# Latent attention: value products on half columns in fp32, with the sums of probabilities on GpSimd

## The chip, the cores and the metric

The program runs on one core of one Trainium2 chip. The metric is the device time of one execution in microseconds, as the median of several executions of the same kernel. TensorE (PE) does the matrix products, VectorE (DVE) and ScalarE (ACT) the elementwise work, GpSimd (POOL) a little of it; SyncE (SP) issues most transfers.

## The reference, cut to what matters

A trunk of two layers over 1024 positions of width 1024. The first layer mixes tokens by multi-head latent attention (12 heads, keys of 64+32, values of 64), the second by a sliding window; both have four cross-attention heads beside them, an output projection and a squared-ReLU MLP. The change lies in the causal attention of the first layer:

```
sc = einsum('bqhd,bkhd->bhqk', q_blk, k) * scale
sc = where(k_idx <= t_idx, sc, NEG)
p  = softmax(sc, axis=-1)
o  = einsum('bhqk,bkhd->bqhd', p, v)
```

The softmax is computed as exp(scores minus the row's maximum), a product with the values, and a division by the sum of the exponentials. All of it has the accuracy of fp32.

## The kernel before

**Tiles.** Scores are computed transposed: a block is 128 keys (on partitions) by up to 512 queries. Group G=0 holds queries 0 to 511, G=1 queries 512 to 1023, so a head has 4 blocks (k=0 to 3) of group 0 and 8 (k=0 to 7) of group 1. A block on the diagonal (k >= 4G) has only the columns from (k-4G)*128 on, so widths are 512, 384, 256 and 128. Step n of the main loop is one block of one head (`seq`, 12 steps a head); the list `blocks` gives the order, `blocks_end` that of the last head.

**A step.** `scores` makes three products into one PSUM bank `pss` (high and low parts of q and k, in the fp32r format), adds the mask on DVE where the block is on the diagonal, and takes the exponential on ACT into `p`. The row's maximum comes in as a 97th row of q, which `row_max` (PE product `psx`, minimum of the negated scores on DVE) and `max_row` (a transpose, a split, two small DMAs) prepare for a later head; the table `WHEN` says at which steps. `head_tiles` loads and splits q and k of the head after next.

**Values.** `values` is called for the block three steps back and, for its second part, five steps back (`LV`, `LB`). Blocks of group 1, and (0, 3) of the first eleven heads, are used whole (`whole`): one fp32 product of `vf` (64 columns of values and 64 of ones) with `p`, so that the lower half of the bank `pso` holds the output and the upper half the sums of probabilities. The other blocks of group 0 are split into `ph` (ACT) and `pl` (DVE) and take three fp32r products with `vh` and `vl`. `v_tiles` and `v_full` make these value tiles for each head.

**After a group.** ACT copies 65 rows of `pso` into `on`; DMAs take the output back into `qn` and the row of sums into `den`. For groups of heads (0 to 5, 6 to 9, 10) `rc_split` takes reciprocals of `den`, writes them to DRAM and reads them back spread over 64 partitions (`rb`, two buffers), in the queue of POOL for the first two groups; `rc_mul` multiplies one output tile in each odd step. The last head is divided straight from PSUM by `last_o`, its group 1 at once, its group 0 in the output projection (`wo_phase`).

**Order.** Each engine works through one queue, in an order fixed when the program is built: a planner takes the instructions by their place in the program and puts each where its inputs and a free buffer are to be had. `tc.issue_after(x)` ties what is issued inside it behind instruction x in the queue of x's engine. A wait at the head of a queue holds up all that stands behind it.

Of the kernel before, what the change touches and what calls it, by code (L numbers as in the profile page):

```python
# [9 lines left out]
F32 = mybir.dt.float32  # L10
# [9 lines left out]
P = 128  # L20
# [35 lines left out]
def trunk(  # L56
# [943 lines left out]
    vbufs = []  # L1000
    for i in range(2):
        vb = (at.tile([P, 4, 128], F32R, name=f"vh{i}"), at.tile([P, 4, 64], F32R, name=f"vl{i}"))
        vbufs.append(vb)
    vfs = [at.tile([P, NT, 128], F32, name=f"vf{i}") for i in range(2)]
    for vf in vfs:
        nc.gpsimd.memset(vf[:, :, 64:128], 1.0)

    def v_tiles(h):

        vh, vl = vbufs[h % 2]  # L1010
        src = v[:, 0:4, h * 64 : (h + 1) * 64]
        if h < 2:
            nc.gpsimd.memset(f32(vh[:, :, 64:128]), 1.0)
        nc.scalar.activation(vh[:, :, 0:64], src, AF.Copy)
        nc.vector.tensor_tensor(vl, src, f32(vh[:, :, 0:64]), ALU.subtract)

    blocks = [(1, 0), (0, 0), (1, 4), (0, 1), (1, 5), (0, 2), (1, 6), (0, 3), (1, 7), (1, 1), (1, 2), (1, 3)]

    def whole(h, G, k):
        return G == 1 or (k == 3 and h < H - 1)  # L1020

    blocks_end = [(1, k) for k in (0, 4, 5, 6, 7, 1, 2, 3)] + [(0, k) for k in range(4)]

# [3 lines left out]
    probs, po_, masked = {}, {}, []  # L1027

    def width(G, k):
        return 512 - max(0, k - 4 * G) * P  # L1030

    def scores(h, G, k):

        qh, ql, kh, kl = bufs_[h % 3]
        c0 = 512 - width(G, k)
        ks = slice(k * P, (k + 1) * P)
        qs = slice(G * 512 + c0, G * 512 + 512)
        diag = k >= 4 * G
        ps = ps1(f"pss{h}_{G}_{k}")[:, c0:]

        def mm(o, a, b, **kw):
            return lambda: nc.tensor.matmul(o, a, b, skip_group_check=True, **kw)  # L1042

        mms = [mm(ps, kh[:, ks], qh[:, qs], start=True, stop=False)]
        mms.append(mm(ps, kh[:, ks], ql[:, qs], start=False, stop=False))
        mms.append(mm(ps, kl[:, ks], qh[:, qs], start=False, stop=True))

        def then():
            if diag:
                masked[0:1] = [nc.vector.tensor_tensor(ps[:, 0:P], ps[:, 0:P], dmaskT, ALU.add).ins]  # L1050
            p = at.tile([P, 512], F32, tag="p", bufs=5, name=f"p{h}_{G}_{k}")
            masked[1:] = [nc.scalar.activation(p[:, c0:], ps, AF.Exp, scale=SC).ins]  # L1052
            if whole(h, G, k):
                probs[(h, G, k)] = p
                return
            ph = at.tile([P, 512], F32R, tag="ph", bufs=3, name=f"ph{h}_{G}_{k}")
            pl = at.tile([P, 512], F32R, tag="pl", bufs=3, name=f"pl{h}_{G}_{k}")
            split(p[:, c0:], ph[:, c0:], pl[:, c0:])
            probs[(h, G, k)] = (ph, pl)

        return mms, then

    def values(h, G, k, late):

        vh, vl = vbufs[h % 2]
        c0 = 512 - width(G, k)
        order = [b[1] for b in blocks_of(h) if b[0] == G]
        first, last = k == order[0], k == order[-1]
        mms = []

        def mm(o, a, b, **kw):
            mms.append(lambda: nc.tensor.matmul(o, a, b, skip_group_check=True, **kw))  # L1072

        if first and not late:
            po_[(h, G)] = ps1(f"pso{h}_{G}")
        po = po_[(h, G)]
        if whole(h, G, k):
            if late:
                return [], lambda: None
            mm(po[:, c0:], vfs[h % 2][:, k, :], probs.pop((h, G, k))[:, c0:], start=first, stop=last)  # L1080
        elif late:
            mm(po[:, c0:], vh[:, k, :], probs.pop((h, G, k, "late"))[:, c0:], start=False, stop=last)
        else:
            ph, probs[(h, G, k, "late")] = probs.pop((h, G, k))
            mm(po[:, c0:], vh[:, k, :], ph[:, c0:], start=first, stop=False)
            mm(po[0:64, c0:], vl[:, k, :], ph[:, c0:], start=False, stop=False)
            last = False

        def then():
            if not last:  # L1090
                return
            r = slice((h % 2) * 64, (h % 2) * 64 + 64)
            if h == H - 1:
                if G:
                    last_o(G, at.tile([64, 512], F32, tag="on", bufs=2, name="rq1"))
                return
            on = at.tile([65, 512], F32, tag="on", bufs=2, name=f"on{h}_{G}")
            nc.scalar.activation(on, po[0:65], AF.Copy)
            nc.sync.dma_start(out=qn[h // 2][r, G * 512 : (G + 1) * 512], in_=on[0:64])
            c = [c for c in range(3) if h >= GRP[c]][-1]  # L1100
            d0 = (h - GRP[c]) * NT + 4 * G
            nc.sync.dma_start(out=den[c][d0 : d0 + 4, :], in_=on[64:65])

        return mms, then

    def last_o(G, tmp, js=range(4)):

        po = po_[(H - 1, G)]
        for j in js:
            c = slice(j * P, (j + 1) * P)  # L1110
            nc.vector.reciprocal(tmp[:, c], po[64:128, c])
            nc.vector.tensor_tensor(qn[5][64:128, G * 512 + j * P : G * 512 + (j + 1) * P], po[0:64, c], tmp[:, c], ALU.mult)
# [7 lines left out]
    def rc_pair(c, j, i):  # L1120

        rb = at.tile([P, 512], F32, tag="rb", bufs=2, name=f"rb{c}_{j}_{i}")
        for e in range(min(2, GRP[c + 1] - GRP[c] - 2 * j)):
            (nc.sync if c == 2 else nc.gpsimd).dma_start(out=rb[e * 64 : e * 64 + 64, :], in_=rc_d[c][2 * j + e, halves[i]].partition_broadcast(64))
        return rb

    def rc_split(c):
# [4 lines left out]
        (nc.sync if c == 2 else nc.gpsimd).dma_start(out=rc_d[c].rearrange("h (t p) -> (h t) p", p=P), in_=rc)  # L1132
# [33 lines left out]
    for n in range(len(seq) + LB):  # L1166
        ms, mv, then = [], [], []
        if n < len(seq):
            ms, then_s = scores(*seq[n])
        for lag, late in ((LB, True), (LV, False)):  # L1170
            if 0 <= n - lag < len(seq):
                a, b = values(*seq[n - lag], late)
                mv += a
                then.append(b)

        mix = []
        if ms and mv and P in [width(*seq[n - lag][1:]) for lag in (0, LV, LB)]:
            while ms and mv:
                mix += [ms.pop(0), mv.pop(0)]
        for f in mix + ms:  # L1180
            f()
        if n < len(seq):
            then_s()
# [1145 lines left out]
```

## Time and profile before

| | before |
|---|---|
| median of 3 runs | 2091.34 us (2090.69 to 2093.28) |
| profiled execution: span from first to last instruction | 2089.8 us |
| PE, weight loads, DVE, ACT, POOL busy, of the span | 99%, 81%, 71%, 53%, 7% |
| score products of the first layer, first to last start | 233.2 to 430.6 us |
| chain that ended last, by engine | PE 94%, DVE 3%, ACT 1%, DMA 1% |

The profile is one execution, and its times are from the span's start. The runs' times hold a little more than the span. Busy PE time is the union of overlapping records, since matrix products are pipelined. A record of the profile is one instruction; a line number is that of the kernel, and names such as `pso<-p,vf` give what is written and read.

### The profile page before, as it was taken

How to read it: one execution, taken by the hardware profiler on the slowest of the kernel's cores; microseconds unless marked ns; L12 is line 12 of the kernel's file. 1: busy time of each engine (PE TensorE's matmuls, PEld its weight loads, DVE VectorE, ACT ScalarE, POOL GpSimd, SP SyncE). 2: the span in 40 equal slices, each digit the busy share in tenths (PEclk: the TensorE clock that was granted, in tenths of full speed). 3: DMA queues.
4: the chain of work that ended last, by engine and by line, in shares of the span. 5: the costliest groups of instructions: out<-in, count | busy, mean ns of one | idle time of the engine just before them, and what ended most of it. 6: DMA issues, size and time to landing. Idle time of an engine off the chain costs nothing.

```text
span 2089.8 us, 28906 instructions
## 1 busy us (share of the span) xinstructions
PE 2072.6 (99%) x9744; PEld 1692.2 (81%) x9744; DVE 1475.7 (71%) x2978; ACT 1109.4 (53%) x2396; POOL 148.6 (7%) x265
## 2 busy tenths in 40 slices
PE   9999999999999999999999999999999999999998
PEld 6988777778888888888888888778888888888887
DVE  8766778775977777976558534666977776976565
ACT  7554466666745544444445435766755544444453
POOL 1001001000000000000001133420000000000000
PEclk9999999999999999999999999999999999999999
DMA  6302223342444546944433534542344446944332
GB/s 225 104 1 77 63 65 93 105 149 81 142 152 150 167 152 233 332 129 152 143 118 108 146 101 124 142 130 84 128 152 164 161 144 233 324 146 156 117 121 91
DMA packets 182228, 292.86 MB, mean 140 GB/s; under 512 B 17739, under 2 KB 72128, under 8 KB 182080
## 3 DMA queue, kind: packets, MB, share of 16 engines
q1 hardware_dynamic: 175584, 272.60, 41.5%
q0 software_dynamic: 5168, 15.80, 2.1%
q10 hardware_dynamic: 1328, 2.63, 0.4%
q8 instruction: 76, 1.25, 0.2%
q14 instruction: 72, 0.59, 0.1%
HBM read 187.60 MB, written 81.44 MB: 129 GB/s over the span
## 4 chain that ended last, share of the span: by engine, by line
PE 94%; DVE 3%; ACT 1%; DMA 1%; issue 1%; SPq 0%; POOL 0%; DVEq 0%; ACTq 0%
PE psy L1903 6%; PE psy L1901 6%; PE psy L1902 6%; PE psu L1565 5%; PE psu L1564 5%; PE psu L1563 5%; PE psz L1903 4%; PE psz L1902 4%; PE psz L1901 4%; PE psv L1565 4%; PE psv L1564 4%; PE psv L1563 4%; PE pso L1072 3%; PE pss L1042 3%; PE pswo L109 3%; PE pswo L111 3%
## 5 line engine op out<-in xcount | busy, mean ns | idle before, releaser
L99 ACT ACTIVATE g<-i 128x512 fp32r<-128x512 f32 x79 | 49.9, 631 | 104.6 <-PE psy L1902 51.8
L1901 PE MATMUL psy<-g 128*128 128x512 f32 x256 | 100.1, 391 | 0.0
L1902 PE MATMUL psy<-g 128*128 128x512 f32 x256 | 99.8, 390 | 0.0
L1903 PE MATMUL psy<-g 128*128 128x512 f32 x256 | 99.8, 390 | 0.0
L1052 ACT ACTIVATE p<-pss 128x512 f32<-128x512 f32 (+2 forms) x144 | 68.7, 486 | 58.5 <-DVE pss L1050 50.0
L100 DVE TENSOR_TENSOR g<-i,g 128x512 fp32r<-128x512 f32 x79 | 55.5, 702 | 51.0 <-ACT g L99 51.0
L1072 PE MATMUL pso<-p,vf 128*128 128x512 f32 (+3 forms) x214 | 87.8, 492 | 0.0
L99 ACT ACTIVATE i<-mr 128x512 fp32r<-128x512 f32 x78 | 47.8, 629 | 73.2 <-PE psy L1902 24.5
L99 ACT ACTIVATE uh<-i 128x512 fp32r<-128x512 f32 x66 | 41.6, 630 | 82.4 <-PE psz L1902 38.4
L100 DVE TENSOR_TENSOR uh<-i,uh 128x512 fp32r<-128x512 f32 x66 | 45.6, 691 | 47.3 <-ACT uh L99 47.2
L916 DVE CUSTOM_DVE_ANT_0 psx<-psx,wide 128x1024 f32<-128x1024 f32 (+6 forms) x88 | 66.7, 760 | 14.6 <-PE psx L909 14.4
L1903 PE MATMUL psz<-g 128*128 128x512 f32 x192 | 74.8, 389 | 0.0
L1901 PE MATMUL psz<-g 128*128 128x512 f32 x192 | 74.8, 389 | 0.0
L1902 PE MATMUL psz<-g 128*128 128x512 f32 x192 | 74.8, 389 | 0.0
L1462 ACT ACTIVATE mr<-mr,gcol 128x256 f32<-128x256 f32 (+1 forms) x160 | 63.9, 477 | 13.9 <-DMA mr<-in_mlp_w_up_dram 13.9
L100 DVE TENSOR_TENSOR i<-mr,i 128x512 fp32r<-128x512 f32 x78 | 53.7, 688 | 24.7 <-ACT i L99 24.7
L1903 PEld LDWEIGHTS psy<-g 128*128 128x128 f32 x256 | 48.1, 188 | 9.9
L1902 PEld LDWEIGHTS psy<-g 128*128 128x128 f32 x256 | 48.1, 188 | 9.8
L1901 PEld LDWEIGHTS psy<-g 128*128 128x128 f32 x256 | 48.1, 188 | 9.8
L1783 DVE TENSOR_TENSOR mqq<-mqf,mqq 128x512 f32<-128x512 f32 x64 | 43.2, 687 | 18.2 <-DMA mqf<-in_mlp_w_down_dram 18.1
L1462 ACT ACTIVATE d<-d,gcol 128x256 f32<-128x256 f32 x128 | 53.6, 499 | 0.1
L2158 ACT ACTIVATE sp<-sp,sst 128x257 f32<-128x257 f32 (+1 forms) x96 | 46.5, 488 | 13.0 <-DVE sst L2156 12.7
(674 smaller groups left out, 6855.4 us busy)
## 6 DMA issues: line engine op xcount, KB each, us to landing
i<-hd SPq DMA_DIRECT2D x154, 256.0 KB
hd<-uh SPq DMA_DIRECT2D x76, 256.0 KB
hd<-ul SPq DMA_DIRECT2D x76, 256.0 KB
mr<-in_mlp_w_up_dram SPq DMA_DIRECT2D x36, 512.0 KB
hd<-x SPq DMA_DIRECT2D x72, 256.0 KB
mr<-hd SPq DMA_DIRECT2D x70, 256.0 KB
d<-in_mlp_w_up_dram SPq DMA_DIRECT2D x32, 512.0 KB
mqf<-in_mlp_w_down_dram SPq DMA_DIRECT2D x32, 512.0 KB
```

The lines of the kernel that those rows point to most:

```text
L99: a = nc.scalar.activation(hi, src, AF.Copy)
L100: d = nc.vector.tensor_tensor(lo, src, f32(hi), ALU.subtract)
L916: nc.vector.tensor_tensor_reduce(o, o, k, -1.0, least, ALU.add, ALU.min, accum_out=m)
L1052: masked[1:] = [nc.scalar.activation(p[:, c0:], ps, AF.Exp, scale=SC).ins]
L1072: mms.append(lambda: nc.tensor.matmul(o, a, b, skip_group_check=True, **kw))
L1462: nc.scalar.activation(w[:, k, :], w[:, k, :], AF.Copy, scale=g_mlp[layer][:, k0 + k : k0 + k + 1])
L1563: nc.tensor.matmul(ps, wh[:, k, :], xh[:, k, :], start=p in (1, 2, 5) and k == 0, stop=False, skip_group_check=True)
L1564: nc.tensor.matmul(ps, wh[:, k, :], xl[:, k, :], start=False, stop=False, skip_group_check=True)
L1565: nc.tensor.matmul(ps, wl[:, k, :], xh[:, k, :], start=False, stop=k == 3, skip_group_check=True)
L1901: nc.tensor.matmul(ps, ah[:, j, :], bh, start=start, stop=False, skip_group_check=True)
L1902: nc.tensor.matmul(ps, ah[:, j, :], bl, start=False, stop=False, skip_group_check=True)
L1903: nc.tensor.matmul(ps, al[:, j, :], bh, start=False, stop=k == NP - 1, skip_group_check=True)
```

## The change

The value products of all blocks take `v` itself (64 columns) and `p` whole in fp32, in pieces of up to 256 query columns. A piece goes to the lower or the upper 64 columns of the array (`quarters`), so one bank `pso` holds both groups of a head. Four blocks form a batch: at every fourth step `values` issues all products of the batch, widest first and alternating between the halves, each tied behind the one before it on PE; the next step's scores and row maxima are tied behind the last of them. The blocks' order is a new one.

POOL adds up the probabilities of a head in `acc` (one add for each block but the first of a group, and a copy of the columns that a narrower second block lacks). `sums` multiplies `acc` by a tile of ones, five steps into the next head, into a bank of its own; ACT copies it to `sm`, and three DMAs take it to `den`. `evac` copies the whole bank `pso` at once, with two DMAs. `v_tiles`, `v_full`, `ph` and `pl` are gone. The transfers of `rc_split` and `rc_pair` all go into SP's queue, `rc_split` comes two steps later and `rc_mul` begins one step earlier. `last_o` divides two query tiles with each reciprocal.

```diff
-    blocks = [(1, 0), (0, 0), (1, 4), (0, 1), (1, 5), (0, 2), (1, 6), (0, 3), (1, 7), (1, 1), (1, 2), (1, 3)]
+    ones = at.tile([P, 64], F32, name="ones")
+    nc.gpsimd.memset(ones, 1.0)
+    blocks = [(1, 0), (0, 0), (1, 5), (0, 1), (1, 4), (0, 2), (1, 1), (1, 6), (1, 2), (0, 3), (1, 7), (1, 3)]
+    BATCH = 4
+    def quarters(G, c0=0):
+        return [(part ^ G, max(c0, part * 256), part * 256 + 256) for part in range(2) if c0 < part * 256 + 256]
     def scores(h, G, k):
...
+        p = at.tile([P, 512], F32, tag="p", bufs=10, name=f"p{h}_{G}_{k}")
+        masked[1:] = [nc.scalar.activation(p[:, c0:], ps, AF.Exp, scale=SC).ins]
...
+        if (h, G) not in first_p:
+            first_p[(h, G)] = p
+            return
+        q = first_p[(h, G)]
+        if q is not None:
+            first_p[(h, G)] = None
+            if c0:
+                nc.gpsimd.tensor_copy(a[:, :c0], q[:, :c0])
+        nc.gpsimd.tensor_tensor(a[:, c0:], p[:, c0:], (a if q is None else q)[:, c0:], ALU.add)
...
+    def values(batch):
+        todo = [[], []]
+        for h, G, k in batch:
...
+            for g, a, b in quarters(G, col0(G, k)):
+                todo[g].append((b - a, po[g * 64 : g * 64 + 64, base + a % 256 : base + a % 256 + b - a], v[:, k, h * 64 : h * 64 + 64], p[:, a:b], g, begun))
+        todo = [sorted(t, key=lambda x: -x[0]) for t in todo]
+        while todo[0] or todo[1]:
+            for t in todo:
+                if t:
+                    _, o, w, r, g, begun = t.pop(0)
+                    with tc.issue_after(last_mm[0]):
+                        last_mm[0] = nc.tensor.matmul(o, w, r, start=g not in begun, stop=True, skip_group_check=True).ins
+                    begun.add(g)
+    def evac(h):
+        po, _ = po_.pop(h)
+        on = at.tile([P, 512], F32, tag="on", bufs=2, name=f"on{h}")
+        nc.scalar.activation(on, po, AF.Copy)
...
+    def sums(h, G=None):
+        acc = acc_[(h, "acc")]
+        sp = ps1(f"psd{h}_{G}")
+        if G is None:
+            acc4 = acc.rearrange("p (a c) -> p a c", c=256)
+            nc.tensor.matmul(sp[0:64].rearrange("p (a c) -> p a c", c=256), ones, acc4[:, 0:4:3, :], start=True, stop=True, skip_group_check=True)
+            nc.tensor.matmul(sp[64:128], ones, acc[:, 256:768], start=True, stop=True, skip_group_check=True)
...
+        nc.scalar.activation(sm, sp[0:65], AF.Copy)
...
-            (nc.sync if c == 2 else nc.gpsimd).dma_start(out=rb[e * 64 : e * 64 + 64, :], in_=rc_d[c][2 * j + e, halves[i]].partition_broadcast(64))
+            nc.sync.dma_start(out=rb[e * 64 : e * 64 + 64, :], in_=rc_d[c][2 * j + e, halves[i]].partition_broadcast(64))
...
+    for n in range(len(seq) + 2):
+        with ExitStack() as queued:
+            if last_mm:
+                queued.enter_context(tc.issue_after(last_mm[0]))
+            if n < len(seq):
+                scores(*seq[n])
+            for g, i in ahead.get(n, ()):
...
+        if n % BATCH == 1 and n > BATCH:
+            values(seq[n - 1 - BATCH : n - 1])
+            if j == 1 and h < H:
+                evac(h - 1)
+            if j == 5 and h:
+                sums(h - 1)
+            if n == len(seq) - 3:
+                sums(H - 1, 1)
+                last_o(1, at.tile([P, 256], F32, tag="on", bufs=2, name="rq1"))
...
+            if n == GRP[c + 1] * NB + 8:
                 rc_split(c)
+            if n == GRP[c + 1] * NB + (11 if c == 2 else 15):
                 muls = rc_mul(c)
+    sums(H - 1, 0)
```

## Rows read from the trace of the kernel before

**Rows 1.** Page, part 1: engine, busy us, share of the span, instructions.

```profile
PE 2072.6 (99%) x9744; PEld 1692.2 (81%) x9744; DVE 1475.7 (71%) x2978; ACT 1109.4 (53%) x2396; POOL 148.6 (7%) x265
```

**Rows 2.** Tile view of `pss`, third pass: min/median/max ns, first and last start.

```profile
L1042 PE MATMUL pss<-qh,kl x96: 223/364/482, 233.7 to 430.6; 97*128 97x512 f32 x48, 97*128 97x384 f32 x16, 97*128 97x256 f32 x16, 97*128 97x128 f32 x16
```

**Rows 3.** Window of one head, all, then `pso` alone: us, busy (xrecords), clock, DMA.

```profile
282.72:299.21 16.49, 16.49 (x79) 12.24 (x78) 12.58 (x32) 10.44 (x22) 0.00 (x0) 1.00 0.29 66
...
282.72:299.21 16.49, 9.85 (x27) 4.66 (x28) 0.00 (x0) 1.18 (x2) 1.00 0.29 66
```

**Rows 4.** Timeline of PE in two places: start, us, instruction, xrecords.

```profile
336.24 0.40 PE L909 MATMUL psx<-ckl,ckh 96*128 96x512 f32 x1
336.47 1.02 PE L1072 MATMUL pso<-p,vf 128*128 128x512 f32 x2
336.93 0.74 PE L1042 MATMUL pss<-qh,kh 97*128 97x384 f32 x1
...
339.54 0.39 PE L1072 MATMUL pso<-ph,vh 128*128 128x512 f32 x1
339.77 0.40 PE L1072 MATMUL pso<-ph,vl 128*64 128x512 f32 x1
340.00 0.28 PE L1042 MATMUL pss<-qh,kh 97*128 97x256 f32 x1
340.12 0.28 PE L1042 MATMUL pss<-ql,kh 97*128 97x256 f32 x1
```

**Rows 5.** Timeline of the windowed layer's value products.

```profile
1334.31 0.28 PE L2151 MATMUL psw<-kh,q 128*128 128x128 f32 x1
...
1334.42 0.27 PE L2152 MATMUL psw<-kl,q 128*128 128x128 f32 x1
...
1334.63 1.51 PE L2204 MATMUL pswo<-spT,v 128*64 128x384 f32 x8
...
1335.00 0.14 PEld L2204 LDWEIGHTS pswo<-spT,v 128*64 128x64 f32 x2 [0.18 <-issue]
...
1335.33 0.14 PEld L2204 LDWEIGHTS pswo<-spT,v 128*64 128x64 f32 x2 [0.18 <-issue]
...
1336.07 0.55 PE L2186 MATMUL pswt<-ident,sp 128*128 128x128 f32 x3
```

**Rows 6.** Lines by form, 233 to 433 us: xcount | busy, mean ns | idle.

```profile
L1098 ACT ACTIVATE on<-pso 65x512 f32<-65x512 f32 x22 | 13.0, 590 | 10.6 <-PE pso L1072 10.5
...
L99 ACT ACTIVATE ph<-p 128x512 fp32r<-128x512 f32 x12 | 7.5, 629 | 0.3
...
L1050 DVE TENSOR_TENSOR pss<-pss,dmaskT 128x128 f32<-128x128 f32 x96 | 29.0, 303 | 6.9 <-PE pss L1042 6.7
...
L916 DVE CUSTOM_DVE_ANT_0 psx<-psx,wide 128x1024 f32<-128x1024 f32 x11 | 13.5, 1228 | 1.9 <-PE psx L909 1.8
...
L100 DVE TENSOR_TENSOR kl<-k,kh 96x1024 fp32r<-96x1024 f32 x7 | 8.5, 1216 | 0.1
...
L100 DVE TENSOR_TENSOR pl<-p,ph 128x512 fp32r<-128x512 f32 x12 | 8.2, 688 | 1.5 <-ACT ph L99 1.5
```

**Rows 7.** Lines by form of POOL, whole span.

```profile
L2176 POOL TENSOR_TENSOR sp<-sp,sst 128x768 f32<-128x768 f32 x28 | 42.0, 1499 | 29.4 <-DVE sst L2175 29.3
...
L1124 POOL DMA_DIRECT2D rb<-rcd x20 | 10.5, 535 | 16.3 <-DVE qn L1141 10.9 <-DMA rcd<-rc 2.9 <-DVE pss L1050 2.5
...
L2176 POOL TENSOR_TENSOR sp<-sp,sst 128x384 f32<-128x384 f32 x4 | 3.3, 829 | 23.3 <-DVE sst L2175 22.3 <-PE psw L2152 1.0
```

**Rows 8.** Waits of PE's weight loads, 233 to 436 us: total, times, longest.

```profile
PEld psx L909 <- DVE m L916: 6.2, 12, 1.1
```

**Rows 9.** Windows at the end of the stretch.

```profile
431.00:436.00 5.00, 4.11 (x18) 2.26 (x16) 4.81 (x10) 4.14 (x13) 0.00 (x0) 0.98 0.95 305
436.00:440.00 4.00, 4.00 (x12) 3.07 (x11) 3.84 (x12) 2.56 (x4) 0.00 (x0) 0.60 0.46 177
```

**Rows 10.** Tile view of `pso`: the last head's reciprocals.

```profile
L1111 DVE RECIPROCAL rq<-pso x4: 958/958/960, 431.5 to 436.5; 64x128 f32<-64x128 f32 x4
```

More of the change, by code (lines that the diff above doesn't have):

```diff
@@ L1061, in scores @@
[L1061 to L1082, printed above, removed]
-        else:
[L1084 to L1104, printed above, removed]
@@ L1106, in last_o @@
-    def last_o(G, tmp, js=range(4)):
-        po = po_[(H - 1, G)]
+        nc.tensor.matmul(ps, kh[:, ks], qh[:, qs], start=True, stop=False, skip_group_check=True)
+        nc.tensor.matmul(ps, kh[:, ks], ql[:, qs], start=False, stop=False, skip_group_check=True)
+        last_mm[0:1] = [nc.tensor.matmul(ps, kl[:, ks], qh[:, qs], start=False, stop=True, skip_group_check=True).ins]
+        if k >= 4 * G:
+            masked[0:1] = [nc.vector.tensor_tensor(ps[:, 0:P], ps[:, 0:P], dmaskT, ALU.add).ins]
@@ new lines, in scores, with bank @@
+        nc.gpsimd.tensor_tensor(a[:, c0:], p[:, c0:], (a if q is None else q)[:, c0:], ALU.add)
+    def bank(h, G):
+        t, n = ((h, G), 1) if h == H - 1 else (h, 2)
+        return t, 256 * G if n == 2 else 0
+    def values(batch):
+        todo = [[], []]
+        for h, G, k in batch:
+            t, base = bank(h, G)
+            if t not in po_:
+                po_[t] = ps1(f"pso{h}_{G}"), set()
+            po, begun = po_[t]
+            p = probs.pop((h, G, k))
+            for g, a, b in quarters(G, col0(G, k)):
[8 more added lines that the diff above has]
+                    begun.add(g)
@@ new lines, in evac @@
+    def evac(h):
+        po, _ = po_.pop(h)
+        r = slice((h % 2) * 64, (h % 2) * 64 + 64)
+        on = at.tile([P, 512], F32, tag="on", bufs=2, name=f"on{h}")
+        nc.scalar.activation(on, po, AF.Copy)
+        dst = qn[h // 2][r, :]
+        nc.sync.dma_start(out=dst.rearrange("p (a c) -> p a c", c=256)[:, 0:4:3, :], in_=on[0:64].rearrange("p (a c) -> p a c", c=256))
+        nc.sync.dma_start(out=dst[:, 256:768], in_=on[64:128])
+    def sums(h, G=None):
[5 more added lines that the diff above has]
+            nc.tensor.matmul(sp[64:128], ones, acc[:, 256:768], start=True, stop=True, skip_group_check=True)
+        else:
+            sp_[G] = sp
+            for g, a, b in quarters(G):
+                nc.tensor.matmul(sp[g * 64 : g * 64 + 64, 0:256], ones, acc[:, G * 512 + a : G * 512 + b], start=True, stop=True, skip_group_check=True)
+            return
+        sm = at.tile([65, 512], F32, tag="sm", bufs=2, name=f"sm{h}")
+        nc.scalar.activation(sm, sp[0:65], AF.Copy)
+        c = [c for c in range(3) if h >= GRP[c]][-1]
+        d0 = (h - GRP[c]) * NT
+        for t, n, src in ((0, 2, sm[0:1, 0:256]), (6, 2, sm[0:1, 256:512]), (2, 4, sm[64:65, :])):
+            nc.sync.dma_start(out=den[c][d0 + t : d0 + t + n, :], in_=src)
@@ L1165, in trunk @@
     muls = iter(())
[L1166 to L1183, printed above, removed]
-        for g, i in ahead.get(n, ()):
-            if i < NT:
-                row_max(g, i)
-            else:
-                max_row(g)
+    for n in range(len(seq) + 2):
[5 more added lines that the diff above has]
+            for g, i in ahead.get(n, ()):
+                if i < NT:
+                    row_max(g, i)
+                else:
+                    max_row(g)
         h, j = divmod(n, NB)
         if n < len(seq):
-            if h + 1 < H and j == 6:
-                with tc.issue_after(masked[1]):
-                    v_tiles(h + 1)
-            if h + 1 < H and j == 8:
-                with tc.issue_after(masked[0]):
-                    v_full(h + 1)
             if h and j == 0 and h + 2 < H:
@@ L1424, in wo_phase @@
                     oo[p + 1] += osp(p + 1, (1,))
-                if layer == 0 and half == 0 and p < 4:
+                if layer == 0 and half == 0 and p < 2:
                     if p == 0:
-                        od = m.t("i39")[0:64, 0, :]
+                        od = m.t("i39")[:, 0, :]
                     last_o(0, od, [p])
```

68 lines of the change are left out of this document (16 added, 52 removed).

## The prediction

> **What bounds the kernel now.** First the busy times of the page: PE works 99% of the span [rows 1], so the first question is whether PE also limits the stretch that changes. The tile view of the score tile gives its place: the third pass of the score products runs from 233.7 to 430.6 us [rows 2], 196.9 us for twelve heads, 16.4 us a head. The window over one steady head says which engine fills it: of 16.49 us PE is busy 16.49, DVE 12.58, ACT 10.44 and POOL 0.00, at a granted clock of 1.00 [rows 3]. So here PE's queue is the time, and a microsecond less of matmul work is a microsecond less of span, until something else is late. The value products are a large part of that queue: 27 records on `pso` a head [rows 3]. Their busy time overlaps the neighbours', so I take pitches (start to start, end to end) instead of durations.
>
> **The value products before, per head.** A product of `p` and `vf` shows as two records. In PE's timeline a 512-column one (x2 at 336.47) stands between a product that ends at 336.24+0.40 = 336.64 and a 384-column one that ends at 336.93+0.74 = 337.67 [rows 4]: 1.03 us for the two. Single-pass products start 0.23 us apart at 512 columns and 0.12 at 256 [rows 4], so 0.17 for the 384-column one is my estimate between them, which leaves 0.86 us, 1.67 ns a column. Group 1 has 5 blocks of 512 columns, then 384, 256 and 128, in all 3328; with the whole block (0, 3) of 128 that is 3456 columns x 1.67 = 5.77 us. The three split blocks of group 0 (512+384+256 = 1152 columns) go three times at 0.23/512 = 0.45 ns: 1.55 us. Sum 7.32 us of the head's 16.5.
>
> **After.** The half-column form is already in this kernel, in the windowed layer (line 2204): 64-column weights, two products side by side on the lower and upper 64 columns of the array. Eight records, four products of 384 columns, take 1.51 us from first start to last end, and the weight loads of one pair stand 0.33 us behind those of the pair before [rows 5]; one after the other the four would need 4 x 384 x 1.67 ns = 2.57 us. So a pair of 384-column products takes two such steps, 0.66 us: 1.72 ns a column for both halves. I counted the quarters that each batch of four blocks gives to either half: 896, 768 and 640 columns on both sides alike, 2304 a head, x 1.72 = 3.96 us. The products of ones with the sums, 512 columns on each half, add 0.88 us.
>
> Then the way in and out. The matmul before the eight starts at 1334.42, 0.11 after one of its kind (1334.31), so 1334.53 was its successor's turn; the first after the eight starts at 1336.07 [rows 5]. That is 1.54 us against 4 x 0.33 = 1.32: 0.22 us a visit. Three visits a head (the ones' products stand behind a batch) make 0.66 us. Beside this stands a rule of the Trainium skill, "TensorEngine Tiling (Array Packing)", section Key Properties: a change of the tiling mode drains the engine. The visit's rows agree; the 64-column product with `vl` at 339.77 does not, 0.23 us from either full-width neighbour [rows 4]. By the rule the sum keeps the 0.66 us, by that row it would lose it.
>
> New values per head: 3.96+0.88+0.66 = 5.50 us, 1.82 less than 7.32; twelve heads 21.8 us. The last head's order leaves its halves uneven (1024 to 640, 896 to 768, 384 to 896 columns; the larger ones sum to 2816, 512 over 2304): 0.9 us back. So PE's work falls by **20.9 us**, to about 14.7 us a head.
>
> **What has to fit into 14.7 us.** ACT and DVE lose work: three `ph` copies a head (0.63 us at 512 columns), three `pl` differences (0.69) [rows 6], the two instructions of `v_tiles` and the copy of `v_full`; `on` stays at two evacuations of one bank (0.59 each [rows 6]), now one for both groups and one for the sums. From 12.58 and 10.44 us [rows 3] both go down, so neither becomes the bound by its total; PE can only be held by their lateness, which is priced below.
>
> GpSimd gets ten adds and two copies of 128 columns a head: in group 1 blocks 4, 1, 2, 3 of 512 columns, then 384, 256, 128, in group 0 384, 256, 128, in all 3584. Its TENSOR_TENSOR takes 1499 ns at 768 columns and 829 at 384 [rows 7]: 1.745 ns a column and 159 ns each. That makes 10 x 0.159 + 3584 x 0.001745 = 7.8 us, and with two copies at most like adds of 128 columns (0.38 each) 8.6 us of 14.7. It hides: the ones' products want a head's sums five blocks after its last block, some 5 us. If the adds came later than that, the excess would stand in PE's queue (rival B). A rule of the Trainium skill speaks against this part: "GPSIMD Engine Reference", section Key points, says that GpSimd shares its SBUF interfaces with VectorE and suffers from VectorE's instructions with two SBUF inputs. No row of this stretch shows such an overlap, POOL being idle here.
>
> **The waits that are added.** Each batch is one block in PE's queue behind the scores of step n, and waits for the exponentials up to step n-2; behind it stand all later scores. Between lie two steps of scores (3 x 0.23 us each at 512 columns, 1.4 us) with row maxima. In a batch the widest go first, so that the late block of the first two batches comes in the third pair, 0.86 us in. The chain to hide is a mask of 0.30 us, an ACT pass over up to 512 columns (0.59, taken from `on`) and at worst a row maximum of 1.23 us ahead of the mask [rows 6]: 2.1 us against 2.26. From below the wait costs nothing; from above, with nothing of the lead left to the mask, about 1 us a batch. PE's wait for row maxima is 6.2 us in all now, 0.5 a head [rows 8]. I take 0.1 us a batch, near that row, 3.6 us in all.
>
> The `rb` and `rcd` transfers move from POOL's queue to SP's: 20 issues of 0.54 us, which on POOL waited 10.9 us for the multiplications that free their buffer [rows 7], and 2 more; evacuation issues 5 a head instead of 4. Behind such a wait on SP stand the loads of a coming head's q and k, the row of maxima and the evacuated outputs. The loads are asked for seven steps before their first use, some 8 us, so I take 1 us; bounds 0 and 10.9.
>
> **The end of the stretch.** From 431 to 436 us PE is busy 4.11 of 5, and from 436 to 440 the granted clock is 0.60, a mix of its levels of 2.4 and 1.2 GHz, after those idle pieces [rows 9]: 0.9 us idle and 4 x 0.4 = 1.6 us lost to the clock. The last head's outputs there hang on four reciprocals of 0.96 us for each group [rows 10]; afterwards two cover it. Against that stands the wait for GpSimd's last adds, up to two of 1.05 us. I take 1 us gained; bounds 2.5 gained and 2 lost.
>
> **Sum**: -20.9 + 3.6 + 1 - 1 = -17.3 us on the profiled span of 2089.8, 2072.5. The median of the runs is 2091.34, 1.5 us above that span; the same difference gives **2074.0 us**. Behind the stretch PE is as full as before (99% [rows 1]), so the gain should reach the end.
>
> **Rivals.**
> (A) The batches wait for their exponentials, in PE's queue. It decides from 1.82/3 = 0.6 us a batch; at 0.75, a mask regularly behind one row maximum, the time is 2091.3 - 20.9 + 36 x 0.75 = 2097. For it: nothing else may fill PE before the batch. Against it: the wide-first order, and DVE's lower load.
> (B) GpSimd's sums pace the heads, by sharing SBUF with DVE, which has about 3 us a head of instructions with two SBUF inputs (`kl` and `ql`, 1.22 each [rows 6], and the scaling by `rb`). If the adds took twice the row's time, 17.2 us a head, that is 0.7 over today's 16.5: 2091.3 + 12 x 0.7 = 2100. Against: 8.6 us at the row's pace, 3 us of overlap at most. The section Key points of the Trainium skill's "GPSIMD Engine Reference" would lead to this rival.
> (C) Nothing waits, the visits cost nothing and the end closes up: 2091.3 - 20.9 - 12 x 0.66 - 2.5 = 2060.
> (D) SP's queue holds up loads and the waits are twice mine: -20.9 + 7.2 + 6 = -7.7, 2083.6.
> (E) The change doesn't do what it says, the two halves run in turn: 2 x 4.84 + 0.66 = 10.3 us a head, 36 us slower, 2127. Four products in 1.51 us speak against it.
>
> **Chances and range.** My forecast 0.53, its own range 2066 to 2081; D 0.18; C 0.14; A 0.08; B 0.05; E 0.02. A measurement of this kernel tells about 0.2%, 4.2 us, from no change. Faster by more than that: the forecast, C and most of D, 0.82; within it 0.06, the rest of D and weak forms of A and B; slower 0.12. The range runs from 2062, just above C, to 2089, the slow cases left out.
>
> **What would show it.** Right: steady heads 14.7 to 15.2 us apart; `pso` records in pairs, 0.21 to 0.23 us from pair to pair at 256 columns; POOL busy 8 to 9 us a head; DVE below 11. Wrong: PE waits of 0.5 us and more at each batch (A); adds well over 1.1 us at 512 columns, and PE waiting for POOL at the ones' products (B); PE waiting for q and k or their splits around the two stretches of `rb` (D). A time above 2089 would mean that the matmul work was not what bounds the heads.

## The result, and the profile after

The changed kernel takes 2096.99 us (median of 8 runs, 2094.45 to 2098.09), beside 2090.93 (2090.43 to 2093.28) for the kernel before on the same chip: a ratio of 1.0026, 95% interval 1.0016 to 1.0036. It is slower by 0.26%; 2074.0 was forecast. Its profiled span is 2096.4 us, 6.6 more than before.

On the page of the kernel after, PE is busy 99% of the span again, as in [rows 1], and that shows nothing. The heads do. These are windows from the first score product of a head to that of the next, for head 0, a steady head, and heads 7 and 8 (columns as in [rows 3]):

```profile
234.22:254.63 20.41, 17.11 (x84) 11.80 (x83) 15.25 (x33) 8.57 (x16) 12.19 (x14) 0.84 0.25 56
...
306.38:323.01 16.63, 15.93 (x95) 10.77 (x94) 11.30 (x27) 8.82 (x18) 11.66 (x13) 1.00 0.28 66
...
356.26:374.80 18.54, 17.49 (x95) 11.46 (x94) 15.36 (x31) 8.63 (x19) 13.57 (x13) 0.91 0.40 105
374.80:393.39 18.59, 17.20 (x95) 11.60 (x94) 12.45 (x29) 8.81 (x18) 11.35 (x13) 0.91 0.46 102
```

Before, the twelve heads start 18.49, 14.55, 16.49, 16.49, 16.47, 16.48, 16.47, 17.44, 16.48, 17.89 and 15.02 us apart; after, 20.41, 18.51, five times 16.62, 18.55, 18.59, 16.18 and 13.36. So the steady heads gain nothing where 1.8 us each were forecast, heads 0 and 1 lose 5.9, heads 7 and 8 lose 3.2, and the last ones give 4.5 back with theirs. The first score product also comes 1.0 us later (234.22 against 233.20); in the runs below it comes anywhere from 233.0 to 234.5, so I take that for scatter. Before, PE was busy in the whole of a steady head [rows 3]; now 0.7 us of it are idle, and POOL is busy for 11.66 where 8.6 were forecast. In three of the windows the granted clock falls below 1.00, and in head 1 it is 0.81.

Lines by form of the kernel after, 250 to 356 us (columns as in [rows 6]):

```profile
L1030 DVE TENSOR_TENSOR pss<-pss,dmaskT 128x128 f32<-128x128 f32 x48 | 15.0, 312 | 25.7 <-PE pss L1028 25.6
...
L100 DVE TENSOR_TENSOR ql<-q,qh 96x1024 fp32r<-96x1024 f32 x4 | 8.1, 2026 | 0.0
L100 DVE TENSOR_TENSOR kl<-k,kh 96x1024 fp32r<-96x1024 f32 x4 | 4.9, 1216 | 0.0
L100 DVE TENSOR_TENSOR ckh<-q,ckh 96x1024 fp32r<-96x1024 f32 x2 | 4.6, 2294 | 0.0
...
L1045 POOL TENSOR_TENSOR acc<-p,acc 128x512 f32<-128x512 f32 x24 | 34.8, 1448 | 14.7 <-ACT mh L99 7.9 <-ACT p L1032 6.3
```

On DVE the low part of q has changed: `ql` takes 2026 ns, and `ckh<-q,ckh`, which is the same instruction for heads 1, 4, 7 and 10, takes 2294, where these differences took 1216 before [rows 6]; `kl`, with the same shape, still takes 1216. The masks, which write to PSUM, keep their time (312 against 303). The 512-column add takes 1448 ns, where 1.05 was worked out. What the longer `ql` does is seen in the timeline of a steady head (start, us, engine, instruction, records, and the idle time ahead with its releaser):

```profile
307.47 1.22 DVE L100 TENSOR_TENSOR kl<-k,kh 96x1024 fp32r<-96x1024 f32 x1
307.54 0.40 PE L1028 MATMUL pss<-ckh,ckl 97*128 97x512 f32 x1
307.72 2.10 POOL L1045 TENSOR_TENSOR acc<-p,acc 128x512 f32<-128x512 f32 x1 [0.96 <-ACT p L1032]
...
308.60 2.29 DVE L100 TENSOR_TENSOR ql<-q,qh 96x1024 fp32r<-96x1024 f32 x1
...
309.40 0.44 PE L1026 MATMUL pss<-ckh,ckl 97*128 97x384 f32 x1
309.68 0.34 PE L1027 MATMUL pss<-ckh,ckl 97*128 97x384 f32 x1
309.85 0.34 PE L1028 MATMUL pss<-ckh,ckl 97*128 97x384 f32 x1
...
310.82 0.28 DVE L1030 TENSOR_TENSOR pss<-pss,dmaskT 128x128 f32<-128x128 f32 x1
...
311.14 0.60 ACT L1032 ACTIVATE p<-pss 128x512 f32<-128x512 f32 x1 [1.03 <-DVE pss L1030]
...
311.76 0.32 DVE L1030 TENSOR_TENSOR pss<-pss,dmaskT 128x128 f32<-128x128 f32 x1
...
312.18 0.49 ACT L1032 ACTIVATE p<-pss 128x384 f32<-128x384 f32 x1 [0.44 <-POOL acc L1044]
...
312.72 0.38 PE L1026 MATMUL pss<-ckh,ckl 97*128 97x256 f32 x1 [0.55 <-ACT p L1032]
```

While POOL adds, and then copies, DVE's `ql` takes 2.29 us instead of 1.22. The scores of the head's second block, whose last product is the one at 307.54, end at 307.94 and get their mask only at 310.82, behind `kl` and `ql`; ACT, idle by then, has waited 1.03 us for it. The mask of the next block (its scores end at 310.2) follows at 311.76, behind a row maximum. The exponential at 312.18 comes behind that mask and behind POOL's copy, which the profile names; both end at 312.09. It ends at 312.67, and PE's score product at 312.72 has waited 0.55 us for it. In head 0 the same chain is longer, and the clock follows:

```profile
243.41 2.23 POOL L1045 TENSOR_TENSOR acc<-p,acc 128x512 f32<-128x512 f32 x1 [1.43 <-ACT p L1032]
...
244.43 2.29 DVE L100 TENSOR_TENSOR kl<-k,kh 96x1024 fp32r<-96x1024 f32 x1
...
246.65 0.28 DVE L1030 TENSOR_TENSOR pss<-pss,dmaskT 128x128 f32<-128x128 f32 x1
...
246.97 0.87 ACT L1032 ACTIVATE p<-pss 128x256 f32<-128x256 f32 x2 [3.70 <-DVE pss L1030]
247.40 0.67 PE L1069 MATMUL pso<-p,v 128*64 128x256 f32 x4 [1.94 <-ACT p L1032]
...
249.88 0.63 PE L1026 MATMUL pss<-qh,kh 97*128 97x512 f32 x1
```

A batch waits 1.94 us for its exponential. Soon after, a 512-column product takes 0.63 us where the rows of before have 0.40 [rows 4]: from 247.9 on, for 13.7 us, the trace grants 1.2 GHz instead of 2.4.

Head 7 has the first chain once more: PE waits 0.89 us for an exponential whose mask stands behind a `ql` of 2.29, and half clock follows, 3.4 us at 364.0. In head 8 the place is another. SP's queue, then PE:

```profile
370.70 0.68 SPq L895 DMA_DIRECT2D qh<-mh  x1
371.77 2.42 SPq L1123 DMA_DIRECT2D rb<-rcd  x4
374.24 0.70 SPq L896 DMA_DIRECT2D ql<-ml  x1
...
376.59 0.50 PE L1027 MATMUL pss<-ql,kh 97*128 97x512 f32 x1 [1.39 <-DMA ql<-ml]
```

Four `rb` transfers, which the change moved to SP, take 2.42 us of its queue between the two small loads that bring the row of maxima to `qh` and `ql`. The first scores of head 8 wait 1.39 us for the second, and half clock follows, 3.4 us at 377.6.

At the end of the stretch the half clock of [rows 9] is gone. But from the end of the last score product to the end of the span it is 1659.3 us, 1659.0 before: nothing was won there.

### The profile page after: what moved, and what is told of

Its sections match the earlier page's. It is cut to its first block, busy times and chain, and to the rows that moved or that the text cites. A ratio compares the mean times of both kernels' runs of the same rounds, so it can differ in the third digit from the quotient of the medians.

```text
span 2096.4 us, 29504 instructions
## 1 busy us (share of the span) xinstructions
PE 2069.5 (99%) x9951; PEld 1677.7 (80%) x9951; DVE 1457.2 (70%) x2913; ACT 1089.0 (52%) x2347; POOL 277.0 (13%) x383
## 4 chain that ended last, share of the span: by engine, by line
PE 92%; DVE 3%; ACT 1%; DMA 1%; issue 1%; SPq 0%; ACTq 0%; DVEq 0%
PE psy L1882 6%; PE psy L1883 6%; PE psy L1884 6%; PE psu L1546 5%; PE psu L1545 5%; PE psu L1544 5%; PE psz L1882 4%; PE psz L1884 4%; PE psz L1883 4%; PE psv L1546 4%; PE psv L1545 4%; PE psv L1544 4%; PE pswo L109 3%; PE pswo L111 3%; PE pswo L110 3%; PE psf L109 2%
## 5 line engine op out<-in xcount | busy, mean ns | idle before, releaser
L1032 ACT ACTIVATE p<-pss 128x512 f32<-128x512 f32 (+3 forms) x144 | 68.4, 489 | 73.0 <-DVE pss L1030 53.2
L1045 POOL TENSOR_TENSOR acc<-p,acc 128x512 f32<-128x512 f32 (+3 forms) x96 | 98.1, 1033 | 38.6 <-ACT p L1032 24.6
L916 DVE CUSTOM_DVE_ANT_0 psx<-psx,wide 128x1024 f32<-128x1024 f32 (+5 forms) x88 | 66.2, 753 | 15.3 <-PE psx L909 15.3
L2002 POOL TENSOR_TENSOR wsr<-wsr,gcol 128x1024 f32<-128x1024 f32 x12 | 23.4, 1950 | 343.9 <-DMA wsr<-in_swa_w_in_dram 317.8
L1069 PE MATMUL pso<-p,v 128*64 128x256 f32 (+1 forms) x480 | 65.4, 384 | 2.9 <-ACT p L1032 2.9
L1030 DVE TENSOR_TENSOR pss<-pss,dmaskT 128x128 f32<-128x128 f32 x96 | 29.4, 308 | 42.0 <-PE pss L1028 40.1
L1884 PEld LDWEIGHTS psy<-g 128*128 128x128 f32 x256 | 48.1, 188 | 10.0
L1882 PEld LDWEIGHTS psy<-g 128*128 128x128 f32 x256 | 48.0, 188 | 9.9
```

The source lines that it names most:

```text
L916: nc.vector.tensor_tensor_reduce(o, o, k, -1.0, least, ALU.add, ALU.min, accum_out=m)
L1045: nc.gpsimd.tensor_tensor(a[:, c0:], p[:, c0:], (a if q is None else q)[:, c0:], ALU.add)
L1882: nc.tensor.matmul(ps, ah[:, j, :], bh, start=start, stop=False, skip_group_check=True)
L1884: nc.tensor.matmul(ps, al[:, j, :], bh, start=False, stop=k == NP - 1, skip_group_check=True)
```

## The experiments

My theory (S in the expectations): DVE's instructions with two SBUF inputs and GpSimd's adds slow each other, and the masks that come late hold up PE. Its rivals: the half-column products themselves cost what was saved, the order tied on PE does it (V), or the queues do (Q).

**1. The adds left out.** The block of adds and copies behind each exponential goes; the sums read a constant tile, so the denominators are not computed.

```
-        nc.gpsimd.tensor_tensor(a[:, c0:], p[:, c0:], (a if q is None else q)[:, c0:], ALU.add)
...
-        acc = acc_[(h, "acc")]
+        acc = acc_c   # memset to 1.0 once
```

> The changed kernel with GpSimd's adds and copies left out (the products of ones read a constant tile, so the division is not the softmax's). Theory S (sharing): in the trace after, DVE's ql difference of two SBUF inputs takes 2.03 us on average and up to 2.29 instead of 1.22 where an add of GpSimd runs beside it, the masks behind it come late, PE waits, and in head 0 the wait of 1.9 us is followed by 13.7 us of half clock. Then without adds ql is 1.22 us again, head 0 has full clock and the time falls by 10 to 18 us, to 2079 to 2087. Theory R (rigid batches): the four score blocks between two batches come too dense for DVE and ACT whatever GpSimd does; steady heads stay at 16.4 to 16.6 us and the time falls by 0 to 4 us, to 2093 to 2097.

2084.57 us (ratio to before 0.9969, 0.9957 to 0.9981): 12.4 less than the changed kernel. A steady head, and head 8; then the line of `ql`, 250 to 356 us:

```profile
298.69:314.23 15.54, 15.42 (x96) 10.79 (x95) 10.23 (x27) 8.81 (x18) 0.00 (x0) 1.00 0.29 70
...
360.97:381.57 20.60, 18.62 (x95) 12.81 (x94) 12.01 (x29) 9.03 (x18) 0.00 (x0) 0.83 0.44 98
```

```profile
L100 DVE TENSOR_TENSOR ql<-q,qh 96x1024 fp32r<-96x1024 f32 x5 | 6.1, 1217 | 0.0
```

`ql` is back at 1217 ns, and a steady head falls by 1.1 us to 15.54, the five of them by 5.4; heads 0 and 1 fall by 5.7 together, at full clock. In the steady heads PE no longer waits for exponentials, with the same batches. That the adds cost this is shown. The wait for `ql` around the `rb` transfers stays: in head 8 PE waits 1.98 us for it, and half clock follows for 6.9. So it is a second cause.

**2. The adds beside the kernel before.** The same adds into a scratch tile that nothing reads, in the kernel before; `on` gets one buffer for room.

```
+            nc.gpsimd.tensor_tensor(a[:, c0:], p[:, c0:], (a if q is None else q)[:, c0:], ALU.add)
...
-tag="on", bufs=2
+tag="on", bufs=1
```

> The kernel before with the change's adds and copies on GpSimd beside it, into one scratch tile that nothing reads (the output's evacuation tile has one buffer instead of two to make room). Theory S: DVE's differences of two SBUF inputs (ql, kl, pl) are stretched by up to 1.1 us each where they meet an add; PE has 0.3 us of slack a head, so each head takes 0.5 to 1.5 us longer, 2097 to 2109. Theory R: sharing is not what costs, 2090 to 2094.

2110.24 us (1.0099, 1.0084 to 1.0114): 19.7 us slower, for work that nobody waits for. The steady head, and one of DVE's lines from 250 us on:

```profile
286.21:303.86 17.65, 16.89 (x79) 12.01 (x78) 13.80 (x32) 10.32 (x22) 11.05 (x12) 1.00 0.27 62
```

```profile
L1015 DVE TENSOR_TENSOR vl<-v,vh 128x256 fp32r<-128x256 f32 x6 | 4.7, 788 | 2.5 <-ACT vh L1014 2.5
```

`vl`, a difference of two SBUF tiles that the change removes, takes 788 ns; before it took 422. The 19.7 lies a little above the range. The single `on` buffer shows no part in it: ACT's copies into `on` wait for PE alone (9.1 us in all, 10.5 before), never for the transfers that free it.

**3. The `rcd` and `rb` transfers back on GpSimd's queue,** but for the last group.

```
-        nc.sync.dma_start(out=rc_d[c]...
+        (nc.sync if c == 2 else nc.gpsimd).dma_start(out=rc_d[c]...
...
-            nc.sync.dma_start(out=rb...
+            (nc.sync if c == 2 else nc.gpsimd).dma_start(out=rb...
```

> The changed kernel with the transfers of the reciprocals (rcd, rb) back in GpSimd's queue. Theory Q (SP's queue): in heads 7 and 8 four rb transfers of 2.4 us stand between the two rows of maxima on SP, the scores of head 8 wait for ql 1.4 us, and half clock follows; without them heads 7 and 8 take 16.6 to 17.2 instead of 18.5 and 18.6 us and the time falls by 3 to 5 us, to 2092 to 2094. Rival: the stretch is late because of DVE's extra work there (two-input multiplications by rb beside the adds); then the two heads stay above 18 us and the time is 2096 to 2099, and GpSimd's adds behind a waiting transfer may make it worse.

2099.84 us (1.0043, 1.0028 to 1.0058). What PE waits for in the last head (total us, times, longest):

```profile
PE psd L1093 <- POOL acc L1045: 3.5, 1, 3.5
```

Heads 7 and 8 fall to 17.4 and 17.1 us, near what theory Q said; but now the adds stand behind transfers in GpSimd's queue (in the last head twice four of them, 2.06 us for each four), PE waits 3.5 us for the last sums, and half clock follows. The last head takes 18.5 us where it took 14.1, and the total is worse. With the adds kept, these transfers hold up something on either queue.

**4. Each batch tied behind the last row-maximum product of its step,** since steady heads cut their third batch in two. The timeline of PE after, at such a place:

```profile
318.90 0.65 PE L1069 MATMUL pso<-p,v 128*64 128x256 f32 x2
319.48 0.67 PE L909 MATMUL psx<-kh,qh 96*128 96x512 f32 x2
320.08 1.51 PE L1069 MATMUL pso<-p,v 128*64 128x256 f32 x10
321.52 0.33 PE L1026 MATMUL pss<-ckh,ckl 97*128 97x128 f32 x1
```

A product shows as two records, 0.2 us from start to start at 256 columns. So one product runs alone (x2, 0.58 us to the next start), then come two row-maximum products, then the other five (x10): two visits where I counted one.

```
+            with tc.issue_after(rm[0]):   # the last psx product
                 values(seq[n - 1 - BATCH : n - 1])
```

> The changed kernel with each batch tied also behind the last row maximum asked for before it, so that no psx product stands inside a batch. In the trace after the third batch of every steady head is cut in two by a row maximum: its first and last products run alone on their half (0.43 us lost) and there is one more way in and out (0.2 to 0.3 us). Theory V (PE's own work is the time of the steady heads): 0.7 us a head, 6 to 8 us less, 2089 to 2091. Rival (lateness of masks and exponentials is the time): no change within 2 us, 2095 to 2099.

2097.16 us (1.0031, 1.0018 to 1.0043): no gain, a miss. A steady head takes 16.61; its timeline of PE:

```profile
318.92 0.68 PE L909 MATMUL psx<-kh,qh 96*128 96x512 f32 x2 [0.49 <-DVE m L916]
319.53 1.52 PE L1069 MATMUL pso<-p,v 128*64 128x256 f32 x12
```

The batch is whole, and PE now waits 0.49 us for DVE's row maximum instead. The cut had filled that wait. Head 7 takes 16.62 us here and head 8 19.76, with the same transfers on SP.

**5. `ql` and `kl` on GpSimd** from head 2 on, so that DVE no longer has these two-input instructions.

```
-        split(q32, qh[0:96], ql[0:96])
-        split(k32, kh[0:96], kl[0:96])
+        nc.scalar.activation(hi, src, AF.Copy)
+        nc.gpsimd.tensor_tensor(lo, src, f32(hi), ALU.subtract)
```

> The changed kernel with the differences ql and kl of heads 2 to 11 computed on GpSimd instead of DVE (the high parts stay on ACT), so that in the steady heads no DVE instruction with two SBUF inputs is left to meet an add. GpSimd's work rises by about 2 x 1.95 us a head (its 1024-column product took 1.94 us in the trace before) to some 12.5 us of a head. Theory S: adds of 512 columns return from 1.45 to 1.05 us, head 0 keeps full clock, steady heads fall from 16.6 to 15.5 to 15.8 us as without adds; heads 7 and 8 stay slow by SP's queue; 2083 to 2089. Rival (GpSimd's own pace): with 12.5 us a head its sums and differences come late, PE waits for them, 2096 or more.

2087.1 us (0.9978, 0.9968 to 0.9987), 9.9 less than the change, with all its work. The steady head, then POOL's line of the widest adds, 250 to 356 us:

```profile
300.06:315.42 15.36, 15.36 (x95) 10.80 (x94) 8.32 (x25) 8.69 (x18) 14.41 (x15) 1.00 0.30 71
```

```profile
L1049 POOL TENSOR_TENSOR acc<-p,acc 128x512 f32<-128x512 f32 x26 | 33.3, 1279 | 2.2 <-ACT mh L99 1.5
```

GpSimd works more, 14.41 us of the head, each add is shorter (1279), and the head is at 15.36, with PE busy in the whole of it. So not the amount of GpSimd's work matters but what DVE does beside it. Heads 0 and 1 still take 16.83 and 18.01 us, with half clock for 6.8, and heads 7 and 8 17.4 and 19.28.

**6. As 5, with the first group's `rcd` and `rb` transfers on GpSimd's queue and whole batches.**

```
+            (nc.sync if c else nc.gpsimd).dma_start(out=rb...
+            with tc.issue_after(rm[0]):
```

> As the run before, with the first group's reciprocal transfers in GpSimd's queue (those of the other groups on SP) and each batch tied behind the last row maximum. Theory S with Q: 2 to 4 us less than the run before by heads 7 and 8, and with DVE's lateness gone the whole batches give back their 0.3 to 0.7 us a head: 2075 to 2083. Rival: GpSimd is too full to issue the transfers and the adds in time, no better than the run before or worse by up to 5 us.

2097.05 us (1.0028, 1.0018 to 1.0038), a miss. In head 7 GpSimd is busy 20.51 of 20.87 us and issues ten transfers besides adds and differences. In heads 7 and 8 DVE waits 7.2 us in all for `rb`, with the masks behind it, and head 8 takes 23.38 us. That GpSimd is too full for the transfers is my reading of this; three things were changed at once.

**7. Without adds (as 1), with `rb` on GpSimd (as 3) and whole batches (as 4).**

> The changed kernel without GpSimd's adds and copies (the products of ones read a constant tile), with the reciprocal transfers of the first two groups in GpSimd's queue and whole batches: what my sum priced, without sharing and without SP's queue. If these two and the cut batches are all that was wrong in the prediction, steady heads take 14.7 to 15.1 us and the time is 2071 to 2076. Rival R (dense score blocks between batches): steady heads stay at 15.4 to 15.6 us and the time is 2077 to 2082.

2083.69 us (0.9964, 0.9951 to 0.9977). A steady head and head 8, and PE's timeline:

```profile
300.93:316.45 15.52, 14.91 (x95) 10.63 (x94) 10.23 (x27) 8.80 (x18) 0.00 (x0) 1.00 0.29 70
...
363.06:379.15 16.09, 15.18 (x95) 10.61 (x94) 11.37 (x29) 8.81 (x18) 0.32 (x1) 1.00 0.41 101
```

```profile
312.92 0.68 PE L909 MATMUL psx<-kh,qh 96*128 96x512 f32 x2 [0.48 <-DVE m L916]
```

Head 8 takes 16.09 us instead of the 20.60 of run 1: with `rb` off SP's queue most of its loss is gone. The steady head stays at 15.52, as the rival said: what the whole batch saves goes into the wait for the row maximum. The total is only 0.9 us below run 1 and above both ranges, since heads 0 and 1 take 17.99 and 17.73 us (17.63 and 15.63 in run 1), with half clock for 6.8.

**8. The order on PE left free:** the ties that queue each value product behind the one before, and those that queue scores and row maxima behind a batch, are dropped.

```
-                    with tc.issue_after(last_mm[0]):
...
-            if last_mm:
-                queued.enter_context(tc.issue_after(last_mm[0]))
```

> The changed kernel with the ties on PE's queue taken out: the planner orders value products, score products and row maxima by their place in the program and their readiness. Theory V: each visit of half-column products costs 0.2 to 0.3 us on the way in and out, and products that lose their partner run alone; more visits make it slower, 2098 to 2110. Rival R: the fixed order is what makes PE wait; without it steady heads fall below 16.2 us and the time to 2085 to 2093.

2097.99 us (1.0033, 1.002 to 1.0046). The steady head:

```profile
302.31:318.84 16.53, 16.53 (x95) 10.64 (x94) 11.65 (x28) 8.66 (x19) 10.70 (x12) 1.00 0.30 66
```

With the order free PE no longer waits in it (busy 16.53 of 16.53), and it still takes 16.53 us. The value products now come in six visits instead of four, three of them one product alone. So the free order takes the waits away and pays for them with lost pairs, as theory V said; it is no cure. Whether another order would be is not tried.

**9. The sharing by itself:** a kernel of its own, with seven groups one behind the other on constant tiles and nothing of the reference.

> A kernel of its own that computes nothing of the reference: groups of DVE instructions alone, GpSimd adds of 128x512 alone, and both at once. DVE: differences of two SBUF tiles of 1024 columns, adds of a PSUM and an SBUF operand of 512, and the row maximum's reduction of a PSUM and an SBUF operand of 1024. Theory S: the two-SBUF difference takes 1.2 us alone and about 2.3 beside adds, the add 1.05 alone and 2.1 beside it; the DVE forms with a PSUM operand and the adds beside them keep their times within 5%. Rival: any DVE work slows GpSimd (and is slowed) alike, so the PSUM forms are stretched too.

The timeline; a group's time by its count is the time of one instruction, from start to start. Then lines by form: the first from 27.7 to 40.7 us, where adds and differences overlap, the second of the whole run (the row maximum, half of them beside adds):

```profile
8.67 7.52 DVE L75 TENSOR_TENSOR d<-a,b 128x1024 f32<-128x1024 f32 x6
...
17.31 7.96 POOL L87 TENSOR_TENSOR q<-e,f 128x512 f32<-128x512 f32 x6
...
26.32 15.81 POOL L87 TENSOR_TENSOR q<-e,f 128x512 f32<-128x512 f32 x8
26.47 13.19 DVE L75 TENSOR_TENSOR d<-a,b 128x1024 f32<-128x1024 f32 x6
...
43.57 6.49 DVE L79 TENSOR_TENSOR d<-ps,b 128x512 f32<-128x512 f32 x9
...
51.16 10.67 POOL L87 TENSOR_TENSOR q<-e,f 128x512 f32<-128x512 f32 x8
52.37 6.48 DVE L79 TENSOR_TENSOR d<-ps,b 128x512 f32<-128x512 f32 x9
```

```profile
L87 POOL TENSOR_TENSOR q<-e,f 128x512 f32<-128x512 f32 x6 | 12.7, 2123 | 0.5
...
L83 DVE CUSTOM_DVE_ANT_0 d<-ps,b 128x1024 f32<-128x1024 f32 x12 | 14.7, 1223 | 0.3
```

Alone, DVE's difference of two SBUF tiles takes 1.25 us and POOL's add 1.33. Together the eight adds take 1.98 on average, but the first and the last of them run almost alone; the six between take 2.12 each, 2.20 from start to start with the pause behind it, and DVE's difference 2.20 too. With one input in PSUM, DVE takes 0.72 alone and beside the adds, its row maximum 1.22, and the adds keep 1.33. This is one execution.

**10. As 5, with the `rb` transfers asked for singly:** two ahead, and one more behind each multiplication.

```
+            if m_ + 2 < len(rt):
+                rt[m_ + 2][2] = rc_pair(c, *rt[m_ + 2][:2])
```

> The kernel with ql and kl on GpSimd, and each rb transfer past the first two asked for only when the multiplication two before it is issued, instead of all at once at the start of the stretch; still on SP. Theory Q: the row of maxima of head 8 no longer waits behind four rb issues (scores waited 1.9 us for qh, half clock for 6.8 us), heads 7 and 8 fall from 17.4 and 19.3 to 16 to 17 us each: 3 to 5 us less than with ql and kl on GpSimd alone, 2081 to 2085. Rival: DVE then waits for the later transfers instead, no gain, 2086 to 2089.

2083.39 us (0.9961, 0.9947 to 0.9974), the lowest median with all the work, ahead of both kernels; its interval touches those of runs 5 and 12. Head 9:

```profile
374.92:394.01 19.09, 17.38 (x95) 11.99 (x94) 14.14 (x27) 10.85 (x21) 18.52 (x18) 0.89 0.49 143
```

Heads 7 and 8 take 16.06 and 15.67 us (17.4 and 19.28 in run 5), as theory Q said. Heads 9 to 11 lose most of it again, 4.3 of the 5.0 us: in head 9 PE waits 1.7 us for DVE's row maximum, and half clock follows. The rest of what the profile gains on that of run 5 lies ahead of the transfers, where all queues hold the same instructions in both: the first score product comes 1.5 us earlier, and heads 0 and 1 are 1.5 us shorter, with half clock for 3.4 us in place of 6.8. So the 3.7 us between the two medians are not the price of SP's queue.

**11. As 5, with the row maxima of head 2 spread later over the blocks.**

```
-        2: ((7, -2), (6, -1), (5, 0), (4, 1), (3, 2), (2, 3), (1, 4), (0, 5), (8, 6)),
+        2: ((7, -2), (6, 0), (5, 2), (4, 4), (3, 5), (2, 6), (1, 7), (0, 8), (8, 9)),
```

> The kernel with ql and kl on GpSimd, and the row maxima of head 2, which stand at four steps in a row, spread over every other step. In heads 0 and 1 PE waits 1.3 us for the one psx buffer and half clock follows for 6.8 us; before the change the value products filled that time. If this is the cause heads 0 and 1 fall from 16.8 and 18.0 to 16.5 and 15.5: 2 to 4 us less, 2083 to 2085. Rival: the clock falls for other idle pieces, no change, 2086 to 2088.

2086.61 us (0.9979, 0.997 to 0.9988). Heads 0 and 1 fall from 16.83 and 18.01 us to 15.54 and 16.20, at full clock, as expected. But heads 7 and 8 go to 19.3 and 19.6, and the total is that of run 5.

**12. Runs 10 and 11 together.**

> Both of the last two edits together with ql and kl on GpSimd, as the version that should beat both kernels. If both causes hold, steady heads of 15.4 us from start to end: 2077 to 2082. If neither does, 2086 to 2089.

2085.7 us (0.9969, 0.9959 to 0.9979), a miss: heads 0 and 1 keep their gain, heads 7 to 9 take 18.6, 19.27 and 17.33. Two edits that each work at their place don't add up. In heads 7 to 9 PE waits for DVE's row maxima (3.8 us in all) and no longer for a load from SP; why they are late in this combination is open.

## Why the prediction was wrong

The step that failed: "It hides", the cost of GpSimd's adds at nothing, with PE "held" only by the lateness of ACT and DVE, which were taken at the durations of a trace in which POOL was idle. That none of those rows showed the overlap was written down and then used as if it spoke for the low end. I did have the mechanism among the rivals (B), but there it could only act by GpSimd's own pace; it acted through DVE. GpSimd has time to spare (11.66 of 16.63 us); what is late is the mask behind a `ql` of 2.0 to 2.3 us. The chain that the prediction priced, "at worst a row maximum of 1.23 us ahead of the mask", also left out what stands there: `kl` and `ql`, 2.4 us by themselves, which PE does not wait for in run 1, and 3.5 beside the adds. And [rows 8], from which the 0.1 us a batch was taken, are waits of weight loads; PE itself was busy in the whole of a steady head [rows 3]. I gave B a chance of 0.05. Point by point, of the 23.0 us between 2074.0 and 2097.0:

- **The adds beside DVE**: 12.4 us by run 1, in the steady heads (16.62 to 15.54) and in heads 0 and 1. Run 5 gets 9.9 of it back with the adds kept. The Trainium skill's "GPSIMD Engine Reference", section Key points, had said that GpSimd shares its SBUF interfaces with VectorE and that VectorE's instructions with two SBUF inputs contend for them; run 9 agrees, and both sides pay (GpSimd 1.33 to 2.20 us, VectorE 1.25 to 2.20).
- **The size of the adds**: 1.05 us forecast at 512 columns, 1.33 measured alone and 1.45 here. The rows at 384 and 768 columns [rows 7] are of another instruction, whose second operand is `sst`; they were no price for this one. By run 5 this pace alone holds up nothing in a steady head.
- **SP's queue** (rival D): 1 us forecast. Head 8 stands 2.0 us above a steady head in the changed kernel and 5.1 in run 1, with the half clock that follows, and run 7 takes 4.5 off there. Asking for the transfers later (run 10) gains 5.0 in heads 7 and 8 and loses 4.3 behind them. It was taken near its low end though the path behind it held the maxima's loads, which I named and priced only as loads with 8 us to spare.
- **The visits**: 0.22 us three times a head. The third batch is cut in two, which the prediction did not count: its first product takes 0.58 us alone and the other five 1.44 (318.90 to 319.48, 320.08 to 321.52), where the whole batch takes 1.45 in run 4. That is 0.6 us for the fourth visit. In the steady head above, the product behind a batch is followed by the next after 0.28 us (309.40 to 309.68) and that one after 0.17, so another 0.1 us of a visit falls on the product behind it, beyond what [rows 5] gave me. So PE's work was mis-sized: 14.7 us a head forecast, 15.36 in run 5, where PE never waits in a steady head. Runs 4 and 7 turn the fourth visit into a wait of 0.48 to 0.49, so this was not won back by any run.
- **The end**: 1 us gained was forecast, none came.

Run 1 takes 12.4 off and still stands 10.6 us above the forecast. Of these, head 8 has 4 beyond the 1 us forecast and the end 1; a steady head takes 15.54, 0.6 over the 15.0 that 16.49 - 1.82 + 0.3 made, some 7 us over twelve heads. With the 12.4 that makes 24, a little more than the 23.0. The parts were not taken off together, so the sum shows that little is missing, and no more: run 7, which has neither adds nor `rb` on SP, still stands 9.7 us above the forecast, with heads 0 and 1 at 17.99 and 17.73 and half clock twice.

Right were the work that falls away (PE's heads go down to 15.36 once DVE is free), pairs side by side (three pairs of products, 12 records, in 1.52 us, run 4), and DVE's and ACT's totals going down. Rival A's wait came (from 284 to 345 us, 3.7 heads, PE waits 2.4 us for exponentials, 0.65 a head; in runs 1 and 5 none), with DVE's sharing as its reason and not the order of the batches. That A's price of 2097 is the measured time is luck: it stood for 0.75 us a batch, and 0.2 came.

## What to carry to other kernels

An idle engine is free only if what it reads does not slow its neighbour: before giving GpSimd element-wise work, count the neighbour's instructions with two SBUF inputs, and ask who waits behind each when it nearly doubles. Where such work must stay, move the colliding instructions too (run 5), or give them an operand in PSUM (run 9 speaks for it; no kernel here tries it). When transfers move to another queue, list the small loads on that queue which the next stage starts with. Asking for the large ones singly freed those loads in run 10, but most of the gain was lost again behind them. And before pricing a batch on PE, look for the products that the order puts inside it.

## What was not expected of the hardware

The sharing depends on the form: DVE's 1024-column difference from 1.25 to 2.20 us, POOL's 512-column add from 1.33 to 2.20 while both work, and nothing at all with one of DVE's inputs in PSUM (0.72 both ways, the row maximum 1.22). And a short wait can cost more than itself: 1.94 us idle in head 0 (3.3 in all its idle pieces) are followed by 13.7 us at 1.2 GHz, in which a 512-column product takes 0.63 us instead of 0.40.
